# The residual parked in DRAM, its place in SBUF lent to four heads' values, and a first sum made by an accumulating DMA

## The chip, the core and the metric

The program runs on one core of a Trainium2 chip. A core has a matmul engine (PE), a vector engine (DVE), an activation engine (ACT), a general engine (POOL), an engine that only issues transfers (SP), and 16 DMA engines that all transfers share. Every engine takes its own instructions strictly in order and waits on semaphores for the others. Data lies in SBUF (128 partitions); PE writes to PSUM; inputs, outputs and scratch lie in DRAM. The metric is the device time of one execution in microseconds (us), as the median over runs.

## The reference

Two layers on a sequence of 512 tokens with 1024 features, all in fp32: a dilated-window attention mixer and a gated feed-forward layer, then an mLSTM mixer and another feed-forward layer, and a final norm. The part that matters here is the attention mixer and the residual around it:

```python
def reference(x, positions, ...):
    h = x
    for i in range(DEPTH):
        if i % N_MIXERS == 0:
            h = h + dilated_attention_mixer(rms_norm(h, attn_norm[j]), positions, attn_w_in[j], attn_w_out[j])
        else:
            h = h + mlstm_mixer(rms_norm(h, mlstm_norm[j]), ...)
        h = h + swiglu(rms_norm(h, ffn_norm[i]), ffn_w_in[i], ffn_w_out[i])
    return rms_norm(h, final_norm)

def dilated_attention_mixer(xn, positions, w_in, w_out):
    proj = (xn @ w_in).reshape(B, S, N_GROUPS, 3, ATTN_HEADS, ATTN_HEAD_DIM)   # 3 groups, 8 heads of 128
    for g, (window, dilation) in enumerate(DIL_CONFIGS):                       # (128,1), (512,4), (2048,16)
        q = apply_partial_rope(proj[:, :, g, 0], positions) * scale
        k = apply_partial_rope(proj[:, :, g, 1], positions)
        v = proj[:, :, g, 2]
        o, lse = dilated_window_attention(q, k, v, window, dilation)
    ...                                                                        # softmax over groups by lse
    return o.reshape(B, S, ATTN_WIDTH) @ w_out
```

## The kernel before

**Layout.** Activations lie feature-major: tile `h[k]` holds 128 features of the residual for all 512 tokens, in an order of tokens that suits the dilations (token 4j+c at place 128c+j). Eight such tiles come from the pool `h`, which has nine buffers of 256 KB. Every fp32 operand of a matmul is split into a high and a low part (ACT writes the high part, DVE the low part, line 209), and a product is three matmuls.

**Attention.** `attention_pair(pr)` does two heads at a time, four pairs in all. For each of the three groups it projects q and k (names a0g0q, a0g0k, a0g1q, ... for pair 0). Weight chunks of 512 KB come on SP's queue into three rotating buffers (tag `wraw`), so SP waits for a buffer before most loads. The values v are made apart from this: in pair 0, after the projections, `values_stage` makes group 0's values for all eight heads and groups 1 and 2's values for the first four heads; pairs 2 and 3 make theirs by themselves (a2g12v, a3g12v).

**The two units.** `values_stage` runs two objects of class `Values`, first `v0_unit` and then `v12_unit`. Each computes a 512 x 1024 by 1024 x 1024 product with Strassen's seven block products (one saved of eight), in the order `V_ORDER`: a11, a12, s1, s2, s4, s3, a22. Each of the seven takes two weight chunks (ch 0 and 1), each of which is split by ACT and DVE; `prepare` does that two chunks ahead of PE. Weight blocks a11 and a21 lie in a tile pair `first` and `own` (tag `pt`, one pair for each ch; the trace calls both v0w or v12w). s1 = a21 + a22 is formed in `own`. The flag `dma_sum` tells how:

- `v0_unit` (`dma_sum` True): an accumulating DMA, issued on POOL's queue, adds a22 into `own` when the unit's loads begin.
- `v12_unit` (`dma_sum` False): a22 is loaded into a `wraw` buffer (v12s_w), and DVE adds it (line 633) when s1 is prepared, or as the order has it, somewhat before.

Later a21 is accumulated into `first` by DMA for s3 (line 642), in both units.

**Natural order.** `v0_unit` writes into two staging tiles `vstage` (tag `v12`, two buffers). Group 0 needs tokens in natural order, so `settle(i, c)` copies quarters of `vstage` into the tile `v0` with four small SBUF-to-SBUF DMAs on POOL's queue, 32 in all of 64 KB each. `v12_unit` writes into two tiles `vq`, which take the two `v12` buffers after the copies have left them. The tile pools, and a scheduler that sets the order on each engine from the dependencies, decide where the copies end up.

**The residual.** `h` is read by `token_forms` (line 557) in pair 0 and then not before the output projection, where `add_to_h` adds to it.

Of the kernel before, what the change touches and what calls it, by code (L numbers as in the profile page):

```python
# [11 lines left out]
F32 = mybir.dt.float32  # L12
# [3 lines left out]
ALU = mybir.AluOpType  # L16
AX = mybir.AxisListType
P = 128

SEQ = 512  # L20
D = 1024
KC = D // P
TB = SEQ // P
# [16 lines left out]
W_BUFS = 3  # L40
# [31 lines left out]
def tile_hybrid_dilated_attn_mlstm(  # L72
# [4 lines left out]
    nc = tc.nc  # L77
# [8 lines left out]
    wp = pool(ctx, "w")  # L86
# [78 lines left out]
    def run(*fns):  # L165
        n0 = len(nc.cur_bb.bb.instructions)
        with tc.issue_after(last_on_pe()):
            for fn in fns:
                fn()
        end = last_on_pe()  # L170
        for ins in nc.cur_bb.bb.instructions[n0:]:
            if ins.engine == end.engine and ins is not end:
                tc.add_manual_dep(end, ins.name, mybir.DependencyInfo(
                    mybir.DependencyClass.NoSync, mybir.DependencyReason.DATA), reason="run")
        fence[0] = end
# [169 lines left out]
    with ExitStack() as actx:  # L345
# [241 lines left out]
        class Values:  # L587


            def __init__(self, name, parts, dest, dma_sum):  # L590
                self.name, self.parts, self.dest, self.dma_sum = name, parts, dest, dma_sum
                self.made = []
                self.todo = [(key, ch) for key, _ in V_ORDER for ch in range(2)]
                self.raw = {}
                self.r = lambda tb: rtok[:, tb:tb + 1]
                self.nr = lambda tb: nrtok[:, tb:tb + 1]
# [13 lines left out]
            def begin(self):  # L610
                for ch in range(2):
                    t = ap.tile([P, 2, 1024], F32, tag="pt", name="%sw%d" % (self.name, ch), bufs=2)
                    self.raw["first", ch], self.raw["own", ch] = t[:, 0], t[:, 1]
                for ch in range(2):
                    self.load("a11", ch, self.raw["first", ch])
                for ch in range(2):
                    self.load("a21", ch, self.raw["own", ch])
                    if self.dma_sum:
                        self.load("a22", ch, self.raw["own", ch], True)

            def prepare(self, n=1):
                for _ in range(n):
                    if not self.todo:
                        return
                    if not self.raw:
                        self.begin()
                    key, ch = self.todo.pop(0)
                    first, own = self.raw["first", ch], self.raw["own", ch]
                    nm = "%s%s%d" % (self.name, key, ch)
                    if key == "s1" and not self.dma_sum:  # L630
                        a22 = wp.tile([P, 1024], F32, tag="wraw", name=nm + "_w", bufs=W_BUFS)
                        self.load("a22", ch, a22)
                        nc.vector.tensor_tensor(own, own, a22, op=ALU.add)
                    if key in ("a12", "a22"):
                        src = self.raw[key, ch] = wp.tile([P, 1024], F32, tag="wraw", name=nm + "_w", bufs=W_BUFS)
                        self.load(key, ch, src)
                    else:
                        src = first if key in ("a11", "s3") else own
                    self.made.append(split_chunk((src, 1024, lambda t: t.rearrange("p (k n) -> p k n", k=2), nm)))
                    if key == "s1":  # L640
                        nc.vector.tensor_tensor(own, own, first, op=ALU.add)
                        self.load("a21", ch, first, True)
                    elif key == "s2":
                        nc.vector.tensor_tensor(own, own, self.raw["a12", ch], op=ALU.add)

            def run(self, following, done=lambda i, tb: None, between={}):
                bank = lambda tag, bufs: [ps.tile([P, 512], F32, tag=tag, name=self.name + "_" + tag, bufs=bufs)
                                          for _ in range(2)]
                banks = {}
                dest, r, nr = self.dest, self.r, self.nr  # L650
                copy = lambda to, src, scale: nc.scalar.activation(to, src, AF.Copy, scale=scale)

                def fold(to, src, scale):
                    nc.vector.scalar_tensor_tensor(to, src, scale, to, op0=ALU.mult, op1=ALU.add)
                for key, okey in V_ORDER:
                    name = {"a11": "c", "a12": "c", "s1": "p", "s4": "p"}.get(key, "u")
                    fresh = name not in banks
                    if fresh:
                        banks[name] = bank(*{"c": ("acc", 3), "p": ("s", 2)}[name])
                    if key in between:  # L660
                        between[key]()
                    for ch in range(2):
                        whl = self.made.pop(0)
                        (self.prepare if self.todo else following)(1)
                        for t in range(2):
                            with fenced():
                                for k in range(2):
                                    for a, b in SPLITS:
                                        nc.tensor.matmul(
                                            banks[name][t], token_tile(okey, a, 2 * ch + k, t), whl[b][:, k],  # L670
                                            start=(fresh and (ch, k) == (0, 0) and (a, b) == SPLITS[0]),
                                            stop=((ch, k) == (1, 1) and (a, b) == SPLITS[-1]), skip_group_check=True)
                    for t in range(2):
                        bk = banks[name][t]
                        if key == "a11":
                            if t == 0:
                                banks["u"] = bank("o", 2)
                            nc.scalar.activation(banks["u"][t], bk, AF.Copy)
                        elif key == "a12":
                            copy(dest(0, t), bk, r(t))  # L680
                            done(0, t)
                        elif key == "s1":
                            copy(dest(1, 2 + t), bk, nr(2 + t))
                        elif key == "s2":
                            copy(dest(0, 2 + t), bk, r(2 + t))
                        elif key == "s3":
                            fold(dest(1, 2 + t), bk, nr(2 + t))
                            done(1, 2 + t)
                        elif key == "s4":
                            fold(dest(0, 2 + t), bk, r(2 + t))  # L690
                            done(0, 2 + t)
                        else:
                            copy(dest(1, t), bk, nr(t))
                            done(1, t)

        def staged_values():
            stage = [ap.tile([P, TB, 512], F32, tag="v12", name="vstage%d" % i, bufs=2) for i in range(2)]
# [7 lines left out]
        def columns(c0):  # L705
            return w_in[:, c0:c0 + 512]

        v0_unit = Values("v0", [columns(2 * D), columns(2 * D + 512)], lambda i, tb: stage[i][:, tb], True)
        v12_unit = Values("v12", [columns(5 * D), columns(8 * D)], lambda i, tb: v_all[1][i][:, tb], False)
        stage, settle = staged_values()  # L710
        nrtok = ap.tile([P, TB], F32, name="nrtok")
        nc.vector.tensor_scalar(nrtok, rtok, -1.0, None, op0=ALU.mult)
# [4 lines left out]
        def values_stage():  # L717
            v0_unit.prepare(2)
            v_all.append(ap.tile([P, TB, D], F32, tag="heads", name="v0"))
            v0_unit.run(v12_unit.prepare, settle, {"a12": forms[2], "s1": forms[3]})  # L720
            vq = [ap.tile([P, TB, 512], F32, tag="v12", name="vq%d" % i, bufs=2) for i in range(2)]
            v_all.append(vq)

            def following(n):
                ready.append(split_chunk(weight_chunk(w_in, len(ready), 256, 4, "a1g0q_k%d" % len(ready))))
            v12_unit.run(following)

        def o_head(k):
            return v_all[0][:, :, k * P:(k + 1) * P]
# [1 line left out]
        def attention_pair(pr):  # L731
# [150 lines left out]
            for g in range(3):  # L882
# [3 lines left out]
                for part in range(2):  # L886
# [23 lines left out]
                    else:  # L910
                        rotate(t, sh, g == 0)
                    qk.append(t)
                    if pr == 0 and 4 <= 2 * g + part:
                        forms[2 * g + part - 4]()
                if pr == 0 and g == 2:
# [9 lines left out]
            for at, fns in zip(RUN_AT[1:] if pr < HEADS // 2 - 1 else LAST_AT, later_runs):  # L925
                defer(at, lambda fns=fns: run(*fns))

            if pr < 2:
                vt.extend(lambda c, i, g=g: v_all[1][g][:, c, (2 * pr + i) * P:(2 * pr + i + 1) * P] for g in range(2))
                return values  # L930
            v12 = ap.tile([P, 2, TB, 256], F32, tag="v12", name=nm + "v12", bufs=2)
            vt.extend(lambda c, i, g=g: v12[:, g, c, i * P:(i + 1) * P] for g in range(2))
# [743 lines left out]
```

## Time and profile before

| | |
|---|---|
| Median of 3 runs | 1437.68 us (1436.86 to 1440.22) |
| The profiled execution, its own time | 1438.73 us |
| Its span, from the first to the last instruction | 1436.8 us |
| Mean granted PE clock | 0.996 |
| First unit on PE | 79.43 to 118.37 us |
| Second unit on PE | 118.37 to 164.75 us |

The span is shorter than the execution's own time by 1.9 us of start and end. In rows of the timeline the first number is the start in the span, the second the duration, both in us; the brackets at a row's end hold how long the engine had stood idle before it and who released it. SPq and POOLq are the issuing queues of SP and POOL; a DMA row's time there is that of issuing, and the transfer's landing is listed apart. In rows of stages there follow, after the stretch and its length, the busy time and count of PE, PE's weight loads, DVE, ACT and POOL, then the granted PE clock, the busy share of the DMA engines and GB/s.

### The profile page before, as it was taken

Reading aid. Unit: us, or ns where it says so; the run is one execution under the profiler, and the core shown is the slowest. Engines: PE = TensorE matmul, PEld = TensorE weight load, DVE = VectorE, ACT = ScalarE, POOL = GpSimd, SP = SyncE. Lnnn points to the kernel's source line nnn. Section 1 sums busy time; section 2 is a strip of 40 time slices with the busy share of each in tenths; the row PEclk is TensorE's granted clock in tenths of the full one; section 3 lists DMA queues with packets and bytes.
Section 4 is the critical chain, followed back from the end, with each engine's and each line's share of the span. In section 5 each row is a group of like instructions: output and inputs, shape, how many; then the busy total and the mean of one; then the engine's idle time right before and its main releaser. Section 6 shows DMA issues by size and latency. Waiting matters only on the chain. (4 is left out here: it accounts for less than half of the span.)

```text
span 1436.8 us, 20238 instructions
## 1 busy us (share of the span) xinstructions
PE 1412.6 (98%) x7968; PEld 1236.6 (86%) x7968; DVE 990.9 (69%) x1699; ACT 621.5 (43%) x1027; POOL 75.1 (5%) x129
## 2 busy tenths in 40 slices
PE   9998999999999999999999999999999999999997
PEld 7786888888888788999988888798888899998886
DVE  7975596865767487778772458987668777786223
ACT  7254532324125343544552233785444344555222
POOL 2013010000101000000000010100000000000101
PEclk9999999999999999999999999999999999999999
DMA  9347344252524424323233233321223333323231
GB/s 280 100 90 173 118 107 154 84 183 88 183 91 123 146 92 129 118 80 98 89 110 95 96 83 88 89 61 58 89 88 101 105 118 118 94 69 118 73 117 59
DMA packets 129878, 156.54 MB, mean 109 GB/s; under 512 B 6836, under 2 KB 112628, under 8 KB 129784
## 3 DMA queue, kind: packets, MB, share of 16 engines
q1 hardware_dynamic: 121936, 132.60, 29.9%
q0 software_dynamic: 6192, 21.54, 5.7%
q8 instruction: 62, 1.02, 0.3%
q10 hardware_dynamic: 1656, 1.12, 0.2%
q14 instruction: 32, 0.26, 0.1%
HBM read 143.18 MB, written 9.96 MB: 107 GB/s over the span
## 5 line engine op out<-in xcount | busy, mean ns | idle before, releaser
L1611 PE MATMUL fin<-fw_h,f1hh 128*128 128x512 f32 (+1 forms) x198 | 72.8, 368 | 0.0
L1611 PE MATMUL fin<-fw_l,f1hh 128*128 128x512 f32 (+1 forms) x198 | 72.5, 366 | 0.0
L1611 PE MATMUL fin<-fw_h,f1hl 128*128 128x512 f32 (+1 forms) x198 | 72.4, 366 | 0.0
L209 DVE TENSOR_TENSOR fw_l<-fw_w,fw_h 128x1024 fp32r<-128x1024 f32 x22 | 27.1, 1233 | 65.5 <-ACT fw_h L208 65.5
L209 DVE TENSOR_TENSOR fo_k_l<-fo_k_w,fo_k_h 128x1024 fp32r<-128x1024 f32 (+1 forms) x24 | 27.2, 1134 | 62.0 <-ACT fo_k_h L208 62.0
L239 PE MATMUL fo<-f0hh,fo_k_h 128*128 128x512 f32 x176 | 68.5, 389 | 0.0
L239 PE MATMUL fo<-f0hl,fo_k_h 128*128 128x512 f32 x176 | 68.5, 389 | 0.0
L239 PE MATMUL fo<-f0hh,fo_k_l 128*128 128x512 f32 x176 | 68.5, 389 | 0.0
L208 ACT ACTIVATE fo_k_h<-fo_k_w 128x1024 fp32r<-128x1024 f32 (+1 forms) x24 | 23.8, 990 | 74.7 <-PE fo L239 74.7
L208 ACT ACTIVATE fw_h<-fw_w 128x1024 fp32r<-128x1024 f32 x22 | 23.3, 1060 | 67.8 <-PE fin L1611 67.8
L1611 PEld LDWEIGHTS fin<-fw_h,f1hh 128*128 128x128 f32 x198 | 37.4, 189 | 6.0
L1611 PEld LDWEIGHTS fin<-fw_h,f1hl 128*128 128x128 f32 x198 | 37.3, 189 | 6.0
L1611 PEld LDWEIGHTS fin<-fw_l,f1hh 128*128 128x128 f32 x198 | 37.4, 189 | 6.0 <-DVE fw_l L209 0.2
L239 PEld LDWEIGHTS fo<-f0hh,fo_k_h 128*128 128x128 f32 x176 | 33.0, 188 | 6.9
L239 PEld LDWEIGHTS fo<-f0hl,fo_k_h 128*128 128x128 f32 x176 | 33.0, 188 | 6.9
L239 PEld LDWEIGHTS fo<-f0hh,fo_k_l 128*128 128x128 f32 x176 | 33.0, 188 | 6.8
L239 PE MATMUL f0j<-n_h,f0j_h 128*128 128x512 f32 x96 | 37.5, 390 | 0.0
L239 PE MATMUL f1j<-n_h,f1j_h 128*128 128x512 f32 x96 | 37.5, 390 | 0.0
L239 PE MATMUL f1j<-n_h,f1j_l 128*128 128x512 f32 x96 | 37.4, 389 | 0.0
L239 PE MATMUL f0j<-n_h,f0j_l 128*128 128x512 f32 x96 | 37.4, 389 | 0.0
L239 PE MATMUL f0j<-n_l,f0j_h 128*128 128x512 f32 x96 | 37.3, 389 | 0.0
L239 PE MATMUL f1j<-n_l,f1j_h 128*128 128x512 f32 x96 | 37.3, 389 | 0.0
(2128 smaller groups left out, 4896.7 us busy)
## 6 DMA issues: line engine op xcount, KB each, us to landing
f0j_w<-in_ffn_w_in_dram SPq DMA_DIRECT2D x28, 512.0 KB, 4.1
f1j_w<-in_ffn_w_in_dram SPq DMA_DIRECT2D x28, 512.0 KB, 3.8
fw_w<-in_ffn_w_out_dram SPq DMA_DIRECT2D x22, 512.0 KB, 3.9
fo_k_w<-in_ffn_w_out_dram SPq DMA_DIRECT2D x20, 512.0 KB, 3.5
awo_k_w<-in_attn_w_out_dram SPq DMA_DIRECT2D x8, 512.0 KB, 6.3
mv_k_w<-in_mlstm_w_in_dram SPq DMA_DIRECT2D x8, 512.0 KB, 3.6
mqk_k_w<-in_mlstm_w_in_dram SPq DMA_DIRECT2D x8, 512.0 KB, 3.7
mo_k_w<-in_mlstm_w_in_dram SPq DMA_DIRECT2D x8, 512.0 KB, 3.6
```

The lines of the kernel that those rows point to most:

```text
L208: nc.scalar.activation(hi[:, :n], raw[:, :n], AF.Copy)
L209: nc.vector.tensor_tensor(lo[:, :n], raw[:, :n], hi[:, :n].bitcast(F32), op=ALU.subtract)
L239: nc.tensor.matmul(acc, whl[a][:, k, m * P:(m + 1) * P], pairs[b][kk], start=(kk == 0 and (a, b) == SPLITS[0]), stop=(kk == nk - 1 and (a, ...
L1611: nc.tensor.matmul(acc[i][:, cs], a[a_][kk][:, tb * P:(tb + 1) * P], whl[b_][:, k, cs], start=(kk == 0 and (a_, b_) == SPLITS[0]), stop=(k ...
```

## The change

1. `dma_sum` goes: both units form s1 by an accumulating DMA on POOL's queue. `v12_unit` loses the two `wraw` loads of a22 and the two additions on DVE.
2. `vq` becomes eight tiles of 128 x 512 from the pool `h`. So that they can lie there, `keep_residual` stores the eight `h` tiles to a DRAM scratch `kept` after a0g1k, and `bring_residual` loads them into new tiles `hx` after the q and k projections of pair 2, the first pair that no longer reads `vq`.
3. `settle` is no longer called when each piece of `v0_unit` is done, but at four points of `v12_unit`: before s2, s4, s3 and a22.

```diff
-            def __init__(self, name, parts, dest, dma_sum):
+            def __init__(self, name, parts, dest):
...
                 for ch in range(2):
                     self.load("a21", ch, self.raw["own", ch])
-                    if self.dma_sum:
-                        self.load("a22", ch, self.raw["own", ch], True)
+                    self.load("a22", ch, self.raw["own", ch], True)
...
-                    if key == "s1" and not self.dma_sum:
-                        a22 = wp.tile([P, 1024], F32, tag="wraw", name=nm + "_w", bufs=W_BUFS)
-                        self.load("a22", ch, a22)
-                        nc.vector.tensor_tensor(own, own, a22, op=ALU.add)
...
-        v0_unit = Values("v0", [...], lambda i, tb: stage[i][:, tb], True)
-        v12_unit = Values("v12", [...], lambda i, tb: v_all[1][i][:, tb], False)
+        v0_unit = Values("v0", [...], lambda i, tb: stage[i][:, tb])
+        v12_unit = Values("v12", [...], lambda i, tb: v_all[1][i][tb])
...
-            v0_unit.run(v12_unit.prepare, settle, {"a12": forms[2], "s1": forms[3]})
-            vq = [ap.tile([P, TB, 512], F32, tag="v12", name="vq%d" % i, bufs=2) for i in range(2)]
+            v0_unit.run(v12_unit.prepare, {"a12": forms[2], "s1": forms[3]})
+            vq = [[hp.tile([P, 512], F32, tag="h", name="vq%d%d" % (i, tb), bufs=KC + 1) for tb in range(TB)]
+                  for i in range(2)]
...
-            v12_unit.run(following)
+            quarters = lambda i, *cs: lambda: [settle(i, c) for c in cs]
+            v12_unit.run(following, {"s2": quarters(0, 0, 1), "s4": quarters(0, 2, 3), "s3": quarters(1, 2, 3),
+                                     "a22": quarters(1, 0, 1)})
+
+        kept = dp.tile([KC, P, SEQ], F32, name="x_kept")
+
+        def keep_residual():
+            for k in range(KC):
+                nc.sync.dma_start(kept[k], h[k])
+
+        def bring_residual():
+            h[:] = [hp.tile([P, SEQ], F32, tag="h", name="hx%d" % k, bufs=KC + 1) for k in range(KC)]
+            for k in range(KC):
+                nc.sync.dma_start(h[k], kept[k])
...
+                    if pr == 0 and 2 * g + part == 3:
+                        keep_residual()
...
+            if pr == 2:
+                bring_residual()
```

A scheduler sets the order on each engine, so the built order tells more than the diff. PE's order is the same but for names and for the smaller `vq` tiles.

DVE, at the start of the second unit (v12a_l is the low half of a chunk of a11 or a12, v12s_l of a sum; v12w the tiles in which the sums are made), before:

```order
L209 TENSOR_TENSOR v12a_l<-v12w_1011,v12a_h 128x1024
L633 TENSOR_TENSOR v12w_1011<-v12w_1011,v12s_w 128x1024
L209 TENSOR_TENSOR v12a_l<-v12w_1012,v12a_h 128x1024
L209 TENSOR_TENSOR v12a_l<-v12a_w,v12a_h 128x1024
L633 TENSOR_TENSOR v12w_1012<-v12w_1012,v12s_w 128x1024
L209 TENSOR_TENSOR v12a_l<-v12a_w,v12a_h 128x1024
L209 TENSOR_TENSOR v12s_l<-v12w_1011,v12s_h 128x1024
```

And now:

```order
L209 TENSOR_TENSOR v12a_l<-v12w_996,v12a_h 128x1024
L209 TENSOR_TENSOR v12a_l<-v12w_997,v12a_h 128x1024
L209 TENSOR_TENSOR v12a_l<-v12a_w,v12a_h 128x1024 x2
L209 TENSOR_TENSOR v12s_l<-v12w_996,v12s_h 128x1024
L636 TENSOR_TENSOR v12w_996<-v12w_996 128x1024
```

The two additions that stood between the splits of a11 and a12 are gone, and the splits follow one another.

POOL, over both units (v0w and v12w are accumulating DMAs, v from vstage the copies to natural order), before:

```order
L606 DMA v0w_738<-in_attn_w_in_dram 128x2x512
L701 DMA v_754<-vstage_352 32x512
L606 DMA v0w_739<-in_attn_w_in_dram 128x2x512
L701 DMA v_754<-vstage_352 32x512 x15
L701 DMA v_754<-vstage_353 32x512 x16
L606 DMA v12w_1011<-in_attn_w_in_dram 128x2x512
L606 DMA v12w_1012<-in_attn_w_in_dram 128x2x512
```

And now:

```order
L606 DMA v0w_747<-in_attn_w_in_dram 128x2x512
L692 DMA v_763<-vstage_352 32x512
L606 DMA v0w_748<-in_attn_w_in_dram 128x2x512
L692 DMA v_763<-vstage_352 32x512 x10
L606 DMA v12w_996<-in_attn_w_in_dram 128x2x512
L692 DMA v_763<-vstage_352 32x512 x2
L606 DMA v12w_997<-in_attn_w_in_dram 128x2x512
L692 DMA v_763<-vstage_352 32x512 x3
L692 DMA v_763<-vstage_353 32x512 x14
L606 DMA v12w_996<-in_attn_w_in_dram 128x2x512
L692 DMA v_763<-vstage_353 32x512
L606 DMA v12w_997<-in_attn_w_in_dram 128x2x512
```

The scheduler still puts eleven copies ahead of the first new accumulate (a22 into a21) and thirteen ahead of the second; the accumulates of a21, which stood behind all copies, now stand behind thirty and thirty-one of them.

SP, in pair 0, around the loads of a0g1q and a0g1k, before:

```order
L608 DMA v0w_738<-in_attn_w_in_dram 128x2x512
L200 DMA a0g1q_k_w<-in_attn_w_in_dram 128x4x256 x2
L200 DMA a0g1k_k_w<-in_attn_w_in_dram 128x4x256
L608 DMA v0w_739<-in_attn_w_in_dram 128x2x512
L200 DMA a0g1k_k_w<-in_attn_w_in_dram 128x4x256
```

And now:

```order
L726 DMA x_kept<-h_98 128x512
L608 DMA v0w_747<-in_attn_w_in_dram 128x2x512
L200 DMA a0g1q_k_w<-in_attn_w_in_dram 128x4x256 x2
L200 DMA a0g1k_k_w<-in_attn_w_in_dram 128x4x256
L726 DMA x_kept<-h_99 128x512
```

The first row is the last of four stores that now follow the loads of a0g0k, the last row the first of four that stand between the two loads of a0g1k; three of the four v0w loads have moved back behind them. Seven of the eight loads of `hx` stand in pair 2 between the third and the last weight chunk of a2g12v, the eighth early in pair 1.

More of the change, by code (lines that the diff above doesn't have):

```diff
@@ L587, in tile_hybrid_dilated_attn_mlstm @@
         class Values:
-            def __init__(self, name, parts, dest, dma_sum):
-                self.name, self.parts, self.dest, self.dma_sum = name, parts, dest, dma_sum
+            def __init__(self, name, parts, dest):
+                self.name, self.parts, self.dest = name, parts, dest
                 self.made = []
@@ L644, in prepare, with run @@
                         nc.vector.tensor_tensor(own, own, self.raw["a12", ch], op=ALU.add)
-            def run(self, following, done=lambda i, tb: None, between={}):
+            def run(self, following, between={}):
                 bank = lambda tag, bufs: [ps.tile([P, 512], F32, tag=tag, name=self.name + "_" + tag, bufs=bufs)
@@ L680, in run @@
                             copy(dest(0, t), bk, r(t))
-                            done(0, t)
                         elif key == "s1":
@@ L687, in run @@
                             fold(dest(1, 2 + t), bk, nr(2 + t))
-                            done(1, 2 + t)
                         elif key == "s4":
                             fold(dest(0, 2 + t), bk, r(2 + t))
-                            done(0, 2 + t)
                         else:
                             copy(dest(1, t), bk, nr(t))
-                            done(1, t)
         def staged_values():
@@ L706, in columns @@
             return w_in[:, c0:c0 + 512]
-        v0_unit = Values("v0", [columns(2 * D), columns(2 * D + 512)], lambda i, tb: stage[i][:, tb], True)
-        v12_unit = Values("v12", [columns(5 * D), columns(8 * D)], lambda i, tb: v_all[1][i][:, tb], False)
+        v0_unit = Values("v0", [columns(2 * D), columns(2 * D + 512)], lambda i, tb: stage[i][:, tb])
+        v12_unit = Values("v12", [columns(5 * D), columns(8 * D)], lambda i, tb: v_all[1][i][tb])
         stage, settle = staged_values()
@@ L926, in attention_pair @@
                 defer(at, lambda fns=fns: run(*fns))
+            if pr == 2:
+                bring_residual()
             if pr < 2:
-                vt.extend(lambda c, i, g=g: v_all[1][g][:, c, (2 * pr + i) * P:(2 * pr + i + 1) * P] for g in range(2))
+                vt.extend(lambda c, i, g=g: v_all[1][g][c][:, (2 * pr + i) * P:(2 * pr + i + 1) * P] for g in range(2))
                 return values
```

## The prediction

> **What bounds the kernel now.** I read the head of the page first, then the waits of PE, then PE's timeline and the stages around its longest wait, and last who waits for what ahead of it.
>
> ```profile
> span 1436.8 us, 20238 instructions
> PE 1412.6 (98%) x7968; PEld 1236.6 (86%) x7968; DVE 990.9 (69%) x1699; ACT 621.5 (43%) x1027; POOL 75.1 (5%) x129
> PE v_acc L669 <- DVE v12a_l L209: 5.0, 1, 5.0
> PE a0g2q L239 <- DVE rot L521: 0.5, 1, 0.5
> ```
>
> PE, the matmul engine, is busy for 98% of the span, so time is won only where PE stands still or runs slowly. The last two rows are waits of PE (total, times, longest): the first one, the largest of the whole kernel, lies in the stage that the change rewrites, in the second unit's first product (a11, tile v12a). PE's timeline shows the hole and what comes after it; the rows of 79.43, 118.37 and 164.75 are the first matmuls of the first unit, of the second and of what follows.
>
> ```profile
> 79.43 0.39 PE L669 MATMUL v_acc<-v0a_h,xa_h 128*128 128x512 f32 x1
> 118.37 0.39 PE L669 MATMUL v_acc<-v12a_h,xa_h 128*128 128x512 f32 x1
> 121.09 0.39 PE L669 MATMUL v_acc<-v12a_h,xa_h 128*128 128x512 f32 x1
> 126.45 0.80 PE L669 MATMUL v_acc<-v12a_l,xa_h 128*128 128x512 f32 x1 [4.97 <-DVE v12a_l L209]
> 127.46 0.63 PE L669 MATMUL v_acc<-v12a_h,xa_h 128*128 128x512 f32 x1
> 127.89 0.63 PE L669 MATMUL v_acc<-v12a_l,xa_h 128*128 128x512 f32 x1
> 164.75 0.39 PE L239 MATMUL a1g0q<-xa_h,a1g0q_k_h 128*128 128x512 f32 x1
> 121.30:126.40 5.10, 0.17 (x1) 0.00 (x0) 2.37 (x3) 1.04 (x1) 1.69 (x4) 0.79 0.29 56
> 126.40:130.90 4.50, 4.45 (x11) 3.53 (x12) 1.35 (x2) 0.58 (x1) 2.23 (x5) 0.50 0.91 214
> ```
>
> The two units issue the same 168 matmuls (7 products of 24). The first takes 118.37 - 79.43 = 38.94 us, the second 164.75 - 118.37 = 46.38 us. The difference, 7.44 us, is what the hole costs: about 5.1 us of standing still, and then matmuls 0.43 us apart (127.46, 127.89) instead of 38.94 / 168 = 0.23, because the granted clock (in the two stage rows the number ahead of DMA share and GB/s) fell to 0.50. The 0.79 of the row ahead says when it fell: about 3 us after PE stopped.
>
> Why DVE was late stands in its own timeline, and behind it the load that it waited for (microseconds from issue to landing, last column):
>
> ```profile
> 124.03 1.22 DVE L633 TENSOR_TENSOR v12w<-v12w,v12s_w 128x1024 f32<-128x1024 f32 x1 [9.29 <-DMA v12s_w<-in_attn_w_in_dram]
> 125.18 1.22 DVE L209 TENSOR_TENSOR v12a_l<-v12w,v12a_h 128x1024 fp32r<-128x1024 f32 x1
> 130.67 1.23 DVE L633 TENSOR_TENSOR v12w<-v12w,v12s_w 128x1024 f32<-128x1024 f32 x1 [3.15 <-DMA v12s_w<-in_attn_w_in_dram]
> 115.85 1.06 ACT L208 ACTIVATE v12a_h<-v12w 128x1024 fp32r<-128x1024 f32 x1 [2.36 <-PE v_o L669]
> v12s_w<-in_attn_w_in_dram SPq DMA_DIRECT2D x1, 512.0 KB, 11.9
> ```
>
> The split that PE needs at 121.3 was ready to run on DVE from 116.9 (ACT's half ends there). It stood in DVE's queue behind the first addition of a22 to a21 (L633), which waited for a load issued at 112.03 and landed 11.9 us later. The data was no use to PE before the third product: the hole is a matter of order on DVE.
>
> **The change part by part.** *DVE loses the two additions of L633.* They cost 2 x 1.22 us of DVE and the waits of 9.29 and 3.15 us in front of them. Without them the split runs at about 117 to 118.2, three microseconds before PE asks for it, and PE goes on. Worth: the 7.44 us above, if nothing else in the unit comes late. What is late next is the data of the third product (s1 = a21 + a22), now summed by an accumulating DMA on POOL's queue.
>
> *When it must land.* In the first unit, which runs without a hole, ACT starts the s1 splits at 85.56 and 87.79, and PE takes the first at 90.31, that is 6.1, 8.4 and 10.9 us after the unit's start. DVE's half of the first ends at 87.87, so the pair takes 2.3 us.
>
> ```profile
> 85.56 1.05 ACT L208 ACTIVATE v0s_h<-v0w 128x1024 fp32r<-128x1024 f32 x1
> 87.79 1.07 ACT L208 ACTIVATE v0s_h<-v0w 128x1024 fp32r<-128x1024 f32 x1 [1.17 <-PE v_acc L669]
> 86.65 1.22 DVE L209 TENSOR_TENSOR v0s_l<-v0w,v0s_h 128x1024 fp32r<-128x1024 f32 x1
> 90.31 0.39 PE L669 MATMUL v_s<-v0s_h,vT 128*128 128x512 f32 x1
> 102.08 1.05 ACT L208 ACTIVATE v0s_h<-v0w 128x1024 fp32r<-128x1024 f32 x1
> ```
>
> Moved to 118.37, PE wants the first half of s1 at 129.25 and the second 2.7 us later; the sums must have landed by about 126.9 and 129.6.
>
> *When it will land.* The order puts the two accumulates on POOL behind 11 and 13 copies to natural order, eight of which went out by 97 us (the last two at 96.03), and each waits for its a21 load. Those loads (the four v12w, from 104.4 on) landed at the latest 10.2 us after issue; the last, issued at about 107.0, so at 117.2.
>
> ```profile
> 104.42 3.02 SPq L608 DMA_DIRECT2D v12w<-in_attn_w_in_dram  x4
> v12w<-in_attn_w_in_dram SPq DMA_DIRECT2D x1, 512.0 KB, 10.2
> v0w<-in_attn_w_in_dram POOLq DMA_DIRECT2D x1, 512.0 KB, 6.1
> v0w<-in_attn_w_in_dram POOLq DMA_DIRECT2D x1, 512.0 KB, 9.9
> 96.03 0.98 POOL L701 DMA_DIRECT2D v<-vstage  x2 [0.46 <-DMA v0w<-in_attn_w_in_dram]
> 107.48 3.90 POOL L701 DMA_DIRECT2D v<-vstage  x8 [10.48 <-DVE vstage L654]
> 116.30 0.50 POOL L701 DMA_DIRECT2D v<-vstage  x1 [4.91 <-DMA v<-vstage]
> q1 hardware_dynamic: 373, 0.71, 64.7%
> q0 software_dynamic: 222, 0.46, 41.3%
> ```
>
> The trace has accumulates of the same size in the first unit: 6.1 us with the engines nearly free (issued at 89.7), 9.9 us beside saturated loads (issued at 22.6). So the second sum lands between 123.3 and 127.1, or, at the pace that POOL's queue had from 112 to 117 (last two rows: 0.46 MB in 5 us), behind a first one landing as late as 125.0 (its load issued by 104.9, then 10.2 and 9.9 us), at 130.7 (0.52 MB more, 5.7 us). The three ends give PE a wait of 0, 0 and 1.1 us. I take 0: the traffic is the same, since POOL's accumulates stand where copies stood in the row of 107.48, and the a22 loads leave SP's queue.
>
> [...]
>
> *Later accumulates and copies.* a21 is then accumulated into a11 for s3, behind 14 more copies. In flight at most eight POOL transfers stood in the trace (the ninth copy of a run starts at 116.30, when the first of 107.48 has landed). Counting on by eights puts these accumulates at 132 to 137, landing by 138 to 147; s3 is split from 141.0 (first unit: the row of 102.08, 22.65 us in) and must be in by 143.4 and 146.2. Central case 0, worst case a few microseconds, together with the late s1.
>
> *The residual kept in DRAM.* Eight stores of 256 KB on SP, four between the loads of a0g0k and a0g1q, four between the two of a0g1k.
>
> ```profile
> 20.11 1.71 SPq L200 DMA_DIRECT2D a0g1q_k_w<-in_attn_w_in_dram  x2
> 29.02 0.37 SPq L200 DMA_DIRECT2D a0g1k_k_w<-in_attn_w_in_dram  x1
> 24.90 0.60 ACT L432 ACTIVATE h<-xT 128x512 f32<-128x512 f32 x1
> 68.58 1.06 ACT L208 ACTIVATE v0a_h<-v0w 128x1024 fp32r<-128x1024 f32 x1 [4.39 <-PE a0g2q L239]
> 34.00:47.00 13.00, 12.52 (x57) 10.04 (x55) 13.00 (x26) 4.13 (x4) 0.00 (x0) 1.00 0.31 63
> ```
>
> SP's loads behind them wait for buffers until 20.11 and 29.02; the last tile of the residual is written at 25.5, so no load is issued later than now. What moves back is 2 MB of v0w, wanted only at 68.58. The price is bounded by -0.3 us (less traffic early, at most part of that 0.5) and by +1 us: DVE is full from 34 to 47, so a late a0g1q split would push PE's 0.5 us wait at a0g2q one for one. I take 0.
>
> *Bringing it back.* One 256 KB load early in pair 1, seven in pair 2, after the last use of vq.
>
> ```profile
> L873 PE MATMUL a1o<-a1pT,vq x32: 275/275/275, 304.5 to 309.5; 128*128 128x128 f32 x32
> 311.00:317.00 6.00, 6.00 (x28) 4.99 (x27) 3.08 (x7) 1.06 (x1) 0.00 (x0) 1.00 0.00 0
> 331.58 1.06 ACT L208 ACTIVATE a2g12v_k_h<-a2g12v_k_w 128x1024 fp32r<-128x1024 f32 x1 [4.61 <-PE a2g12v L297]
> ```
>
> They can start at 309.8, in a stretch in which the DMA engines moved nothing. 1.8 MB at the 214 GB/s of the slow-clock row is 8.6 us, so done by 319; the one weight chunk behind them is wanted at 331.58. Cost 0. The residual is read again after 480 us.
>
> Sum: -7.44 + 0 + 0 + 0. The profiled execution took 1438.73 us (1.05 above the median of 1437.68); it becomes 1431.3, and the median 1430.3. PE's order is unchanged elsewhere, and what follows hangs on PE, so the gain is not eaten later.
>
> **The rivals.** *The sums land late, a small new wait* (0 to 3 us at s1 or s3, clock kept): 1430.3 to 1433.3. For it the 130.7 above, against it the 6.1 row. [...] *They land over 3 us late*: the clock falls again, costing the same 2.3 us (7.44 less 5.1); a wait of 3.1 us leaves 7.44 - 3.1 - 2.3 = 2.0 us, so 1435.7. The second sum would land at 132.7, 15.5 us after 117.2; no accumulate here took over 9.9. *Slower:* POOL holds the accumulates behind the copies so long that PE stands 8.5 us or more at s1 (8.5 + 2.3 - 7.44 = 3.4, so 1441); it decides from a landing at 138, 21 us after issue. It would need the copies' 8.8 us batches ahead of both accumulates, and the order shows only three and five unsent ones there. *The hole only moves:* the split of a11 finds ACT or a load late instead. ACT's half starts at 115.85, released by PE, so no: a wait of 5 us there would give 1437.7.
>
> **How the numbers follow.** A change of 0.2% is 2.9 us, about what a measurement here can tell from none. No new wait, 0.57; small new wait, 0.23 (both faster); over 3 us late or the hole moved, 0.12 (same); slower 0.08. Faster 0.80, same 0.12, slower 0.08. The range runs from 1429.0 (a microsecond of spread under the sum) to 1436.0, which takes in the late case of 1435.7; above it stay the moved hole and the slower case, some 0.13, below it little.
>
> **What the profile after would show.** The v12 unit 39 us long; no row "v_acc <- v12a_l"; the clock at 1.00 throughout it; no L633; DVE's second v12a_l split near 117. Wrong if PE waits for v12s_h or v12s_l with ACT waiting for a DMA on v12w, if a0g2q's wait is over 1.5 us, or if PE's a2g12v waits for a load.

## The result, and the profile after

The changed kernel takes 1431.23 us (median of 6 runs, 1430.62 to 1433.9) against 1438.37 us of the kernel before, run beside it: a ratio of 0.9953, 95% interval 0.9941 to 0.9966 (estimated from all the runs, so not exactly the quotient of the medians). I had forecast 1430.3. The profiled execution took 1431.08 us, its span went from 1436.8 to 1428.8 us. The head of the page and two rows of PE's waits (total, times, longest) of the kernel after:

```profile
span 1428.8 us, 20252 instructions
PE 1410.0 (99%) x7968; PEld 1234.9 (86%) x7968; DVE 988.5 (69%) x1697; ACT 621.3 (43%) x1027; POOL 78.1 (5%) x131
PE a3o L873 <- DMA a3pT<-a3pD: 1.7, 1, 1.7
PE a0g2q L239 <- DVE rot L521: 0.5, 1, 0.5
```

The row "v_acc <- DVE v12a_l" with its 5.0 us, which headed this list, is gone, and the wait at a0g2q is as it was. PE's timeline, the first matmuls of the first unit, of the second and of what follows, and the two stretches in which PE stood still and then ran slowly before (the granted clock is the number ahead of DMA share and GB/s):

```profile
79.36 0.39 PE L664 MATMUL v_acc<-v0a_h,xa_h 128*128 128x512 f32 x1
118.28 0.39 PE L664 MATMUL v_acc<-v12a_h,xa_h 128*128 128x512 f32 x1
157.22 0.39 PE L239 MATMUL a1g0q<-xa_h,a1g0q_k_h 128*128 128x512 f32 x1
121.30:126.40 5.10, 5.10 (x24) 4.24 (x23) 2.14 (x3) 3.09 (x4) 2.49 (x6) 1.00 0.70 137
126.40:130.90 4.50, 4.50 (x21) 3.71 (x21) 3.97 (x4) 3.30 (x4) 4.43 (x10) 1.00 0.52 118
```

The second unit takes 157.22 - 118.28 = 38.94 us, as long as the first of before to the hundredth, and 7.44 less than it took. Of the 8.0 us by which the span is shorter the rest is 0.09 ahead of the unit and 0.5 in PE's wait at a3o (2.2 before, 1.7 now). That wait lies anywhere between 1.0 and 2.5 in the other profiles of this document, so the half microsecond need not come from the change.

Why nothing in the unit is late, from the timelines of DVE, ACT and POOL, with the landings of two transfers (last column, us from issue):

```profile
116.85 1.23 DVE L209 TENSOR_TENSOR v12a_l<-v12w,v12a_h 128x1024 fp32r<-128x1024 f32 x1 [2.17 <-ACT v12a_h L208]
111.44 1.26 POOL L606 DMA_DIRECT2D v12w<-in_attn_w_in_dram  x1 [2.55 <-DMA v12w<-in_attn_w_in_dram]
v12w<-in_attn_w_in_dram POOLq DMA_DIRECT2D x1, 512.0 KB, 8.8
115.72 1.26 POOL L606 DMA_DIRECT2D v12w<-in_attn_w_in_dram  x1 [1.96 <-DMA v12w<-in_attn_w_in_dram]
v12w<-in_attn_w_in_dram POOLq DMA_DIRECT2D x1, 512.0 KB, 8.3
124.47 1.05 ACT L208 ACTIVATE v12s_h<-v12w 128x1024 fp32r<-128x1024 f32 x1
126.64 1.07 ACT L208 ACTIVATE v12s_h<-v12w 128x1024 fp32r<-128x1024 f32 x1 [1.12 <-PE v_acc L664]
129.57 1.26 POOL L606 DMA_DIRECT2D v12w<-in_attn_w_in_dram  x1
130.86 1.75 POOL L606 DMA_DIRECT2D v12w<-in_attn_w_in_dram  x1
140.93 1.05 ACT L208 ACTIVATE v12s_h<-v12w 128x1024 fp32r<-128x1024 f32 x1
```

The split that PE asks for at 121.2 runs on DVE at 116.85. The sums land at 111.44 + 8.8 = 120.2 and 115.72 + 8.3 = 124.0, and ACT splits them at 124.47 and 126.64, in neither case released by a transfer. The a21 accumulates for s3 leave at 129.57 and 130.86 and land 6.1 and 8.3 us later, the second at 139.2, ahead of their first split at 140.93. The residual comes back where the DMA engines had been nearly empty before (a share of 0.00 in the row of 311.00 in the prediction; here the timeline of SP's queue and a stretch):

```profile
302.28 3.61 SPq L731 DMA_DIRECT2D hx<-x_kept  x7
302.00:308.00 6.00, 6.00 (x29) 4.97 (x29) 1.65 (x4) 1.08 (x2) 0.00 (x0) 1.00 0.91 262
```

### The profile page after: what moved, and what is told of

It is laid out like the page before. It is cut to its first block, busy times and chain, and to the rows that moved or that the text cites. A ratio compares the mean times of both kernels' runs of the same rounds, so it can differ in the third digit from the quotient of the medians.

```text
span 1428.8 us, 20252 instructions
## 1 busy us (share of the span) xinstructions
PE 1410.0 (99%) x7968; PEld 1234.9 (86%) x7968; DVE 988.5 (69%) x1697; ACT 621.3 (43%) x1027; POOL 78.1 (5%) x131
```

## The experiments

Medians of one kernel scatter by a microsecond or two between sets of runs (1437.09 to 1438.78 for the kernel before, 1431.23 to 1432.90 for the changed one), so the length of the second unit on PE, from its first matmul to the first of a1g0q, is the sharper measure, though it is that of one execution, the profiled one. The wait of 0.42 us at v_o, which stands in every kernel, is left out of the table. The ratios are estimated from all the runs and lie up to 0.001 off the quotients of the medians.

| run | second unit, us | PE's waits in it | median, us (runs) | before on that chip | ratio, 95% interval |
|---|---|---|---|---|---|
| before (first profile) | 46.38 | 4.97 | 1438.37 (6) | | |
| after | 38.94 | none | 1431.23 (6) | 1438.37 | 0.9953 (0.9941 to 0.9966) |
| sum_alone | 40.79 | 0.47 + 0.76 | 1435.22 (12) | 1438.52 | 0.9986 (0.9976 to 0.9996) |
| copies_early | 44.20 | 2.35 + 0.76 | 1435.24 (12) | 1438.52 | 0.9986 (0.9974 to 0.9998) |
| sum_undone | 46.90 | 4.76 | 1437.29 (11) | 1438.52 | 0.9992 (0.9984 to 1.0001) |
| add_later | 40.10 | 0.76 | 1432.34 (5) | 1438.52 | 0.9961 (0.9949 to 0.9973) |
| after_again | 38.94 | none | 1432.37 (6) | 1438.78 | 0.9961 (0.9948 to 0.9974) |
| delay3 | 40.55 | 1.31 | 1432.94 (6) | 1438.78 | 0.9967 (0.9955 to 0.9980) |
| delay4 | 44.44 | 3.58 | 1437.82 (10) | 1438.78 | 0.9997 (0.9987 to 1.0007) |
| delay6 | 47.47 | 6.10 | 1440.20 (10) | 1438.78 | 1.0013 (1.0004 to 1.0023) |
| one_held | 38.94 | none | 1431.45 (5) | 1437.09 | 0.9968 (0.9956 to 0.9981) |
| after_beside | 38.94 | none | 1432.90 (11) | 1437.09 | 0.9971 (0.9962 to 0.9980) |
| stores_twice | 45.96 | 3.94 | 1436.88 (8) | 1437.09 | 0.9999 (0.9989 to 1.0009) |

**Is the hole a matter of order on DVE?** Two runs: the sum undone in the changed kernel, and the additions only put later in the kernel before.

sum_undone (after, with the `dma_sum` flag and its three places brought back):

```diff
-                    self.load("a22", ch, self.raw["own", ch], True)
+                    if self.dma_sum:
+                        self.load("a22", ch, self.raw["own", ch], True)
...
+                    if key == "s1" and not self.dma_sum:
+                        a22 = wp.tile([P, 1024], F32, tag="wraw", name=nm + "_w", bufs=W_BUFS)
+                        self.load("a22", ch, a22)
+                        nc.vector.tensor_tensor(own, own, a22, op=ALU.add)
```

> The changed kernel with the sum undone: a22 of the second unit is loaded again by SP and added by DVE; the rest of the change stays (residual in DRAM, vq in its place, copies in the second unit's later half). Theory (the hole is DVE's addition standing ahead of the split that PE needs): the wait of PE on v12a_l is back with about 5 us and the clock of 0.50 behind it: 1438.4, all of the gain gone. Rival (later copies free the DMA engines, so that a22 lands sooner than the 11.9 us of before): the first addition starts sooner by what the load gains; with the 8.9 us of an accumulate after the change in place of 11.9 the wait is 2 us, the clock stays, 1433.2.

The hole is back in full (PE's waits, DVE's timeline, and one row of POOL's; behind it the same row of POOL in the kernel before):

```profile
PE v_acc L669 <- DVE v12a_l L209: 4.8, 1, 4.8
124.64 1.23 DVE L633 TENSOR_TENSOR v12w<-v12w,v12s_w 128x1024 f32<-128x1024 f32 x1 [9.08 <-DMA v12s_w<-in_attn_w_in_dram]
124.89 4.03 POOL L697 DMA_DIRECT2D v<-vstage  x8 [3.58 <-DMA v<-vstage]
```

```profile
124.71 3.98 POOL L701 DMA_DIRECT2D v<-vstage  x8 [3.88 <-DMA v<-vstage]
```

The load is as late as ever, landing 11.7 us after issue (11.9 before). This does not test the rival, though: the program asks for the copies later, but POOL sent all 32 of them in the order of before and within a microsecond of the same times (the last eight in the two rows above), so whether later copies would bring the load in sooner stays open. It also means that of the other two parts only the second is left in this run. Without the first part they move the median by 1.2 us, with an interval that includes no gain.

add_later (before, one line):

```diff
-                        nc.vector.tensor_tensor(own, own, a22, op=ALU.add)
+                        behind(lambda: nc.vector.tensor_tensor(own, own, a22, op=ALU.add), engine=DVE)
```

> The kernel before with one edit: DVE's additions of a22 to a21 are put behind the splits of a11 and a12 in DVE's order; everything else (the loads by SP, copies, residual) stays. Theory (the hole was a matter of order on DVE, the data early enough): no wait on v12a_l; the second a22 load still goes out only when the first addition frees its buffer (at 125.3), lands at 130.6, its addition ends at 131.9, 2.3 us after ACT should have begun the split: a wait of PE of 2 to 2.5 us at s1, the clock kept: 1433.3. Rival A (a wait of 2.3 us is enough to pull the clock down): 1435.6. Rival B (the additions themselves, not their order, cost the time): 1438.4, with the wait moved to s1.

One line of order brings 6.28 of the 7.44 us of the unit, and 6.2 us of the median, with the same loads, additions and copies as before. Timelines of DVE, ACT and PE:

```profile
124.17 1.22 DVE L633 TENSOR_TENSOR v12w<-v12w,v12s_w 128x1024 f32<-128x1024 f32 x1
130.22 1.23 DVE L633 TENSOR_TENSOR v12w<-v12w,v12s_w 128x1024 f32<-128x1024 f32 x1 [1.22 <-DMA v12s_w<-in_attn_w_in_dram]
131.53 1.06 ACT L208 ACTIVATE v12s_h<-v12w 128x1024 fp32r<-128x1024 f32 x1 [2.10 <-DVE v12w L633]
133.91 0.51 PE L669 MATMUL v_s<-v12s_l,vT 128*128 128x512 f32 x1 [0.76 <-DVE v12s_l L209]
```

The first addition now finds its data there (no bracket); the second waits for the load that left only when the first had freed its buffer, and PE loses 1.16 us at s1. I had put this wait at 2.0 to 2.5; the unit began 0.65 us later in this run than in the profile I reckoned from, and the load landed 4.7 us after issue instead of 5.3. The clock stayed at 1.00 (all stretches from 79.4 to 157.2).

**Do the copies ahead on POOL matter?** sum_alone takes the first part only; copies_early is the changed kernel with `settle` called as each piece is done.

```diff
-        v12_unit = Values("v12", [...], lambda i, tb: v_all[1][i][:, tb], False)
+        v12_unit = Values("v12", [...], lambda i, tb: v_all[1][i][:, tb], True)
```

> The kernel before with its first part alone: a22 is added to a21 of the second unit by the accumulating DMA on POOL's queue; the residual stays where it is, vq stays in the buffers of vstage, the copies to natural order are issued as soon as their pieces are done. Theory (the copies ahead on POOL decide): 24 copies now stand ahead of the two accumulates, 16 of which went out by 111.4 us and eight at 116.3 to 120.8 before; the accumulates go out at about 124.7 and land 6.1 to 8.9 us later, at 130.8 to 133.6, against a deadline of 126.9. PE waits 3.9 to 6.7 us at s1, the clock falls again (2.3 us), and the gain of 7.4 is gone: 1437.4 to 1440.2, central 1439, so no faster than before. Rival A (an accumulate passes the copies at no cost, the sum itself is the whole gain): 1431.2, no wait at s1. Rival B (the sums are in time, but ACT's write of vq waits for the copies out of vstage's buffers): a new wait of 1 to 3 us later in the unit, 1432 to 1434.

```diff
...
-            v0_unit.run(v12_unit.prepare, {"a12": forms[2], "s1": forms[3]})
+            v0_unit.run(v12_unit.prepare, settle, {"a12": forms[2], "s1": forms[3]})
...
-            v12_unit.run(following, {"s2": quarters(0, 0, 1), ...})
+            v12_unit.run(following)
```

> The changed kernel with one part undone: the copies to natural order are issued as soon as their pieces are done, as before, so that 24 copies instead of 11 and 13 stand ahead of the first accumulates of the second unit on POOL; vq lies in the residual's place and the residual in DRAM. Theory (the order on POOL is what the delay of the copies is for): accumulates issued at about 124.7 instead of 111.4 and 115.7, landed at 130.8 to 133.6, PE waits 3.9 to 6.7 us at s1 and the clock falls: 1437.4 to 1440.2, central 1439. Rival (POOL's queue was never near a limit): 1431.2, no wait at s1. The difference to the run with the sum alone is the price of vq in the buffers of vstage: 0 by theory, 1 to 3 us where vq waits for copies.

In both, 24 copies stand ahead of the a22 accumulates, which leave at 123.22 and 124.46 instead of 111.44. First sum_alone (POOL, ACT, PE), then copies_early (the same, and half a microsecond of its stages):

```profile
123.22 2.48 POOL L606 DMA_DIRECT2D v12w<-in_attn_w_in_dram  x2 [3.18 <-ACT v12a_h L208]
129.40 1.06 ACT L208 ACTIVATE v12s_h<-v12w 128x1024 fp32r<-128x1024 f32 x1 [4.12 <-DMA v12w<-in_attn_w_in_dram]
130.51 0.50 PE L669 MATMUL v_s<-v12s_h,vT 128*128 128x512 f32 x1 [0.47 <-ACT v12s_h L208]
131.78 0.51 PE L669 MATMUL v_s<-v12s_l,vT 128*128 128x512 f32 x1 [0.76 <-DVE v12s_l L209]
```

```profile
124.46 2.48 POOL L606 DMA_DIRECT2D v12w<-in_attn_w_in_dram  x2 [4.38 <-ACT v_o L673]
130.44 1.06 ACT L208 ACTIVATE v12s_h<-v12w 128x1024 fp32r<-128x1024 f32 x1 [6.00 <-DMA v12w<-in_attn_w_in_dram]
131.55 0.50 PE L664 MATMUL v_s<-v12s_h,vT 128*128 128x512 f32 x1 [2.35 <-ACT v12s_h L208]
134.00:134.50 0.50, 0.50 (x4) 0.37 (x3) 0.06 (x2) 0.50 (x2) 0.22 (x2) 0.59 0.28 49
```

The issue time came out as expected (124.7 said, 123.2 and 124.5 measured), and with it the wait at s1. Its size did not: I took a landing 6.1 to 8.9 us after issue and a clock that always falls, and ACT had the data 6.2 and 6.0 us after the first issue. In the profile of sum_alone PE stood 1.2 us and the clock held (1.00 from 118 to 158); in that of copies_early it stood 3.1 us in two pieces and the clock fell (0.59 in the row of 134.0, 0.50 up to 137.5). Among the 12 runs of copies_early eight lie between 1433.3 and 1435.8 and four between 1437.6 and 1441.9; of the 12 of sum_alone nine lie between 1433.6 and 1436.5 and three between 1438.6 and 1440.2. That the slow ones are those in which the clock fell is likely, but not shown: the one profile of copies_early (1438.26 us, with the fall) is from its slow group, the one of sum_alone (1433.64 us, without) is its fastest run. For the same reason the two unit lengths, 40.79 and 44.20 us, do not compare the two kernels; the medians do, and they are the same within 0.02 us. Both kernels end half way: POOL's order, which the third part of the change sets, is worth some 3 us (1435.2 against the 1432.37 of after_again). And the second part, the residual in DRAM and `vq` in its place, in which these two kernels differ, shows neither a cost nor a gain by itself that medians with this scatter could tell.

**Then is the residual's move needed?** one_held is sum_alone, with the 16 copies of the second staging tile held until after the accumulates:

```diff
+            held = []
+            def done(i, c):
+                settle(i, c) if i == 0 else held.append(c)
-            v0_unit.run(v12_unit.prepare, settle, {"a12": forms[2], "s1": forms[3]})
-            vq = [ap.tile([P, TB, 512], F32, tag="v12", name="vq%d" % i, bufs=2) for i in range(2)]
+            v0_unit.run(v12_unit.prepare, done, {"a12": forms[2], "s1": forms[3]})
+            vq = [ap.tile([P, TB, 512], F32, tag="v12", name="vq0", bufs=2)]
...
+            def release():
+                for c in held:
+                    settle(1, c)
+                vq.append(ap.tile([P, TB, 512], F32, tag="v12", name="vq1", bufs=2))
...
-            v12_unit.run(following)
+            v12_unit.run(following, between={"a12": release})
```

> The run with the sum alone, and one thing more: the second half's 16 copies to natural order (vstage1) are held until the second unit's second product, so that only 16 copies, all sent by about 111.4 us, stand ahead of the two accumulates on POOL. The residual is not moved, vq stays in vstage's buffers (vq1 is taken once the held copies are issued). Theory (only the copies ahead of the accumulates count; the moved residual and vq's place buy nothing but the leave to delay copies): accumulates issued at about 116 to 117, landed at 122 to 126 against the deadline of 126.9, no wait at s1, second unit about 39 us: 1431.2 to 1432.4, as the changed kernel. Rival A (vq1 must be free: the held copies land at 135 to 137, vq1 is first written at 133.5, ACT stands up to 3 us and its splits behind it are late): unit 40 to 42 us, 1433 to 1435. Rival B (accumulates still late as with the sum alone): 1435.2.

> The changed kernel on the same chip as the run with one half held, to compare the two. Every theory: 1431.2 to 1432.4.

No. The sums leave together at 115.88; the first lands 7.3 us after its issue, and ACT splits it at 124.89 without waiting for a transfer (POOL's timeline, the landing, ACT's timeline):

```profile
115.88 2.48 POOL L606 DMA_DIRECT2D v12w<-in_attn_w_in_dram  x2 [4.17 <-issue]
v12w<-in_attn_w_in_dram POOLq DMA_DIRECT2D x1, 512.0 KB, 7.3
124.89 1.05 ACT L208 ACTIVATE v12s_h<-v12w 128x1024 fp32r<-128x1024 f32 x1
126.84 2.48 POOL L701 DMA_DIRECT2D v<-vstage  x5 [2.89 <-DMA v12w<-in_attn_w_in_dram]
127.05 1.07 ACT L208 ACTIVATE v12s_h<-v12w 128x1024 fp32r<-128x1024 f32 x1 [1.12 <-PE v_acc L669]
```

The second sum lands by 126.84, when POOL's copies go on, 0.2 us before ACT, released by PE, turns to it: later than in the changed kernel (9.6 us after its issue), but in time. The unit is 38.94 us long, and the median is 1431.45 against 1432.90 of the changed kernel on the same chip; the intervals overlap, so the two can't be told apart here. 4 MB of traffic and the whole second part of the change can be left out.

**Do the stores cost anything?** stores_twice writes the residual to two scratch tensors in the kernel before:

```diff
+            for k in range(KC):
+                for again in range(2):
+                    nc.sync.dma_start(kept[again][k], h[k])
```

> The kernel before with the residual written to DRAM twice (16 stores of 256 KB, 4 MB, on SP's queue in the places of the change's eight, and not read back). Theory (the stores cost nothing, since the queue and the DMA engines have room until PE asks at a0g2q): first matmul of the first unit at 79.4 as before, PE's wait at a0g2q 0.5 us, 1438.4. Rival (eight stores cost the up to 1 us that I allowed for): twice that, first matmul at 81.4 and 1440.4.

The first unit begins at 80.27, 0.84 us later than in the first profile; but so it does in sum_alone, without any store (80.06), and the wait at a0g2q is the same 0.5 (PE's timeline and waits of stores_twice, then PE's timeline of sum_alone):

```profile
80.27 0.39 PE L669 MATMUL v_acc<-v0a_h,xa_h 128*128 128x512 f32 x1
PE a0g2q L239 <- DVE rot L521: 0.5, 1, 0.5
```

```profile
80.06 0.39 PE L669 MATMUL v_acc<-v0a_h,xa_h 128*128 128x512 f32 x1
```

The median of 16 stores stands 0.2 us under that of none, and its interval leaves room for 1.3 us more. Eight cost nothing that can be measured.

**What does a stop of PE cost?** The changed kernel, with DVE making the low half of the second a11 split three, four or six times more, so that PE waits for it as it did before:

```diff
-        nc.vector.tensor_tensor(lo[:, :n], raw[:, :n], hi[:, :n].bitcast(F32), op=ALU.subtract)
+        for m in (n, *again):
+            nc.vector.tensor_tensor(lo[:, :m], raw[:, :m], hi[:, :m].bitcast(F32), op=ALU.subtract)
```

> The changed kernel itself, beside which the three runs with a delayed split are read. Every theory: 1431.2, the second unit 38.94 us long, no wait of PE in it over 0.5 us.

> The changed kernel in which DVE makes the lower half of the second a11 split of the second unit three times more (same result), so that it ends at about 122.9 instead of 118.1 and PE, which asks at 121.2, waits about 1.7 us. Theory (the clock falls only some 3 us after PE stopped): the wait alone is paid, 1432.9, clock 1.00 behind it. Rival A (any stop of PE pulls the clock down for the 2.3 us that it cost before): 1435.2. Rival B (the price of the clock grows with the wait, 2.3 us for 5.0): 1433.7.

> As the run with three, with four repetitions: a split of a12 gets in between in DVE's order, the lower half ends at about 125.4, PE waits about 4.2 us. Theory (fixed price of 2.3 us beyond 3 us): 6.5 us, 1437.7, clock about 0.5 for 4 to 5 us behind the wait, as in the kernel before. Rival A (the wait alone): 1435.4. Rival B (price in proportion to the wait): 1437.3, not to be told from the theory here, but in the run with three.

> As the run with three, with six repetitions: the lower half ends at about 127.8, PE waits about 6.6 us. Theory (fixed price of 2.3 us beyond 3 us): 8.9 us, 1440.1. Rival A (the wait alone): 1437.8. Rival B (price in proportion to the wait): 3.0 us for the clock, 1440.8.

PE's timeline at the end of the wait, in delay3, delay4 and delay6:

```profile
122.98 0.50 PE L666 MATMUL v_acc<-v12a_l,xa_h 128*128 128x512 f32 x1 [1.31 <-DVE v12a_l L210]
```

```profile
126.21 0.50 PE L666 MATMUL v_acc<-v12a_l,xa_h 128*128 128x512 f32 x1 [3.58 <-DVE v12a_l L210]
```

```profile
128.46 0.80 PE L666 MATMUL v_acc<-v12a_l,xa_h 128*128 128x512 f32 x1 [6.10 <-DVE v12a_l L210]
```

Waits of 1.31, 3.58 and 6.10 us make the unit 1.61, 5.50 and 8.53 us longer, so 0.3, 1.9 and 2.4 us come on top: the short stop kept the clock (1.00 from 118 to 135 in delay3), the others paid about the price that I had read off the kernel before (7.44 - 4.97 = 2.5 with the wait of the row). A price for any stop (2.3 in delay3) is refuted, and so is none at all. A price that grows with the wait is refuted too: in sum_undone and stores_twice waits of 4.76 and 3.94 us make the unit 7.96 and 7.02 us longer, so 3.2 and 3.1 us come on top, more than in delay6. How long the clock is low shows in half-microsecond stretches around its fall and its return, of the kernel before, of delay4, delay6, sum_undone and stores_twice:

```profile
124.00:124.50 0.50, 0.00 (x0) 0.00 (x0) 0.47 (x1) 0.00 (x0) 0.00 (x0) 0.74 0.04 8
131.00:131.50 0.50, 0.50 (x4) 0.41 (x3) 0.50 (x1) 0.04 (x1) 0.00 (x0) 0.93 0.06 8
```

```profile
127.00:127.50 0.50, 0.50 (x3) 0.36 (x2) 0.00 (x0) 0.00 (x0) 0.50 (x2) 0.66 0.52 131
130.50:131.00 0.50, 0.50 (x4) 0.43 (x3) 0.00 (x0) 0.50 (x2) 0.50 (x2) 0.93 0.57 139
```

```profile
126.00:126.50 0.50, 0.00 (x0) 0.00 (x0) 0.50 (x1) 0.00 (x0) 0.50 (x2) 0.76 0.35 82
133.00:133.50 0.50, 0.50 (x4) 0.41 (x3) 0.00 (x0) 0.31 (x1) 0.00 (x0) 0.92 0.00 0
```

```profile
126.00:126.50 0.50, 0.00 (x0) 0.00 (x0) 0.50 (x1) 0.00 (x0) 0.50 (x2) 0.90 0.30 74
133.00:133.50 0.50, 0.50 (x3) 0.36 (x3) 0.31 (x1) 0.50 (x1) 0.00 (x0) 0.78 0.81 74
```

```profile
125.00:125.50 0.50, 0.00 (x0) 0.00 (x0) 0.50 (x2) 0.00 (x0) 0.50 (x2) 0.94 0.00 0
132.00:132.50 0.50, 0.50 (x3) 0.46 (x2) 0.17 (x1) 0.50 (x1) 0.00 (x0) 0.74 0.58 123
```

A mean of 0.74 over 0.5 us is 0.24 us at 1.00 and 0.26 at 0.50, so the clock fell at 124.24; by the same reckoning it came back at 131.07. In delay4 it fell at 127.16 and came back at 130.57, in delay6 at 126.26 and 133.08, in sum_undone at 126.40 and 133.22, in stores_twice at 125.44 and 132.26. It is low for 6.83, 3.41, 6.82, 6.82 and 6.82 us, and for 3.41 in copies_early (134.09 to 137.50): once or twice 3.41. It was once where PE was running again when the clock fell (delay4, copies_early), and twice in the four where PE still stood. What these stops cost beyond their length is about half the time that PE ran in that: in the kernel before PE is back at 126.45, (131.07 - 126.45) / 2 = 2.3 us; in delay4 3.41 / 2 = 1.7; in delay6 (133.08 - 128.46) / 2 = 2.3; in sum_undone, with PE back at 127.06, and stores_twice, at 126.25, 3.1 and 3.0. So the price of the clock is no fixed one: it was 1.9 to 3.2 us here, by how long PE ran in the low spell.

In delay4 PE had run again for 127.16 - 126.21 = 0.95 us when the clock fell; in the kernel before it had stood for 124.24 - 121.48 = 2.8 us (121.48 is 126.45 less the wait of 4.97) and was still standing.

## Why the prediction was right

- **The hole is worth 7.44 us.** The unit lost 7.44 in the profile, and 38.94 us stand in all four profiles without a late sum or split (after, after_again, one_held, after_beside). The two other profiles with the hole give 7.96 and 7.02. The medians, less exact, give 7.14, 6.41 and 4.19 on three sets of runs, where the kernel before itself had medians from 1437.09 to 1438.78. Of the 0.9 us by which the first median lies above the forecast 0.7 is in the start: the forecast went from 1437.68, the median of three runs, and six gave 1438.37. Why the other two sets lie 2.1 and 2.6 us above it stays open. The three profiled executions with the hole were slower than their kernels' medians, by 0.4, 2.4 and 1.7 us, and those of the changed kernel were faster, by 0.2, 0.8 and 1.1, so the hole may be smaller in the median execution than in the profiled ones; no profile of another execution shows it.
- **A matter of order on DVE.** Shown by add_later: 6.28 us of the unit from order alone.
- **When the sums must land and do land.** The second was to land between 123.3 and 130.7 and landed at 124.0, the first at 120.2, 6.7 and 5.6 us ahead of the deadlines of 126.9 and 129.6. That late sums would be the danger was right too: held back to 123 and 124 us by copies they cost 1.9 and 5.3 us of the unit. The rival of a wait of 3.1 us, put at 3.1 + 2.3 = 5.4, stands almost so in copies_early, with 3.11 and 5.26. I had judged that the copies ahead matter, but not said that the third part of the change is what keeps them away; the runs show that some 3 us of the gain need it.
- **The small new wait.** It had 0.23, and none of the three profiles of the changed kernel has a wait at s1. The sums landed at 120.2 and 124.0, where the additions of before had found their data at 124.03 and 130.67 (the rows of L633). The second load of before had been held not by the DMA engines but by its buffer: the first addition freed that at 124.03 + 1.22 = 125.25, and the load left at 125.28 and landed 5.3 us later (in add_later it left at 125.4 and landed 4.7 us later). Why the first sum took 8.8 us from issue where the first load had taken 11.9 no run shows.
- **The late accumulates of a21.** Forecast to leave at 132 to 137, they left at 129.57 and 130.86: counting POOL's transfers by eights was too slow: from 124.60 on ten copies and the first accumulate left without a pause. Cost 0, as said.
- **The residual.** Stores 0: the first unit began at 79.36, against 79.43 before, and sixteen stores showed no cost. The loads left at 302.28, where 309.8 less 7.44 had been forecast, and moved at 262 GB/s; no wait of PE at a2g12v appeared.
- **The clock.** "About 3 us after PE stopped" was one instance: 2.8 before, but 4.5 in delay4 and 3.9 in delay6. The price of 2.3 us was one instance as well, of 1.9 to 3.2. For this change neither made a difference.

## What to carry to other kernels

When an engine is late, look at what stands ahead in its queue, and whether it is needed sooner: here a line of order recovers most of what a rearrangement of memory, traffic and queues did. When a transfer with a deadline goes onto a queue that also carries bulk copies, count the copies ahead of it; delaying half of them was the part of this change that mattered beside the sum, and it could be had without moving the residual. Where medians scatter by microseconds, read such edits from the length of the stage in the trace as well, but remember that a trace is one execution: sum_alone and copies_early have the same median and stages 3.4 us apart.

## What was not expected of the hardware

In six profiles the clock's low spells came in lengths of 3.41 and 6.82 us, not in proportion to the stop: stops of PE of 1.3, 3.6, 3.9, 4.8, 5.0 and 6.1 us made the stage 1.6, 5.5, 7.0, 8.0, 7.4 and 8.5 us longer. The clock also fell after PE had gone on: 0.95 us after in delay4, and in copies_early 2.5 us after the first matmul that followed the long wait. Accumulating DMAs of 512 KB in the second unit landed 5.8 to 10.5 us after issue over all the profiles. The first took 8.8 us with 11 copies ahead of it in POOL's queue (after), and 6.1 and 5.9 us with 24 (sum_alone, copies_early): what the copies delayed was the issue.
